# Gated linear attention: keys and queries of a tile in one strip, and score products on 64 rows

## The chip, the cores and the metric

The kernel runs on one core of a Trainium2 chip. The metric is device time in microseconds (us): the time of one launch on that core, as a median over runs. The core's engines are named as the profile names them: PE (TensorE; PEld is its weight load), DVE (VectorE), ACT (ScalarE), POOL (GpSimd) and SP (SyncE, which here only issues transfers).

## What is computed

One layer of a streaming encoder over 1024 prompt frames and 64 frames of a running stream: a normalisation with conditioning, one input projection, two groups of heads side by side (latent attention and gated linear attention), an output projection and a feed-forward block. The change lies in the gated linear attention, of 4 heads with 64 key columns each. Its reference, for a chunk of tokens (`b` is the running sum of the logarithms of the forget gates):

```
    def step(state, xs):
        qc, kc, vc, ac = xs
        b = jnp.cumsum(ac, axis=1)
        decay = jnp.exp(jnp.where(causal, b[:, :, None] - b[:, None, :], -jnp.inf))
        scores = jnp.einsum('bthk,bshk,btshk->bths', qc, kc, decay)
        o = (jnp.einsum('bths,bshv->bthv', scores, vc)
             + jnp.einsum('bthk,bhkv->bthv', qc * jnp.exp(b), state))
```

The decay depends on the query t, the key s and the column k at once, so that the scores are no plain matrix product. Between a key s and a later query t with any reference token m between them, the decay is exp(b[t] - b[m]) times exp(b[m] - b[s]), and each factor can be put on one operand.

## The kernel before, in words

**Tiles and levels.** `gla()` works through nine tiles: eight of 128 prompt tokens and one of the 64 sample frames. In a tile the pairs (s, t) with s < t are covered by levels with half-widths hf = 64, 32, 16, 8, 4, 2, 1 (seven levels, six in the sample tile). In a level the tile is cut into blocks of 2*hf tokens; the keys are the first half of each block, the queries the second half, and the reference token is the last of the first half. A level's matmuls multiply all keys of the tile with all queries of the level, and a predicated copy with a mask of the level takes the valid pairs out of the bank into the score tile `ST`. The diagonal is put in by L698 to L703.

**One level before.** `prep(hf)` makes the operands: the difference for keys on DVE (L659) and that for queries on POOL (L660), one exponential over both on ACT (L661), then the keys' product on DVE into `KL` (L664) and the queries' product into `QL` (L668), for the 64 rows of even heads on DVE and for the 64 rows of odd heads on POOL. Two heads lie on the 128 rows of an operand (the index c tells which two). `QL` is block-structured: its free half j holds the queries of head j on that head's 64 rows and zeros on the others. So one matmul over all 128 rows (L722) gives both heads' scores side by side: 128 columns of weights (the keys), 128 moving columns (2 heads by 64 queries), two such matmuls a level, into one bank `g`. One predicated copy of 128x256 (L725) takes them out. An fp32 matmul stands in the trace as two records of PE and two of PEld.

**Order.** The code is written as generators (`gla`, `main`, `latents`, `gates`, the weight loader) that `interleave` steps in turn by rough costs given in the yields; the framework then schedules each engine's program, so that the order on an engine follows from neither alone. An engine works strictly in its order. Operands are prepared two levels ahead (`ready`), a tile's first two levels during the tile before (`begin`). `KL`, `QL` and `dd` have three buffers, the PSUM pools `g` (`psG`) and `tp` (`psT`) two banks each. `tp` serves transposes: of the gate inputs (L573), of the decayed keys (L733), of the outputs (L780).

**Beside it.** While `gla()` runs, `main()` gives PE the big projections: mm3 (L93 to L95) is a product of split fp32 operands in three matmuls, with 264 to 384 moving columns. The gates' logits come from a small matmul over 33 rows (L578). The running state is updated in L739 to L750, the output made in L762 and L766. The elementwise product `qe` (L706) is on POOL.

**Where q and k come from.** `qk()` computes the projections A0 (queries) and A1 (keys) and ACT writes them to `gqk` (L498 to L514), laid out as four strips of all tokens: two of queries, two of keys.

Of the kernel before, what the change touches and what calls it, by code (L numbers as in the profile page):

```python
# [19 lines left out]
P = 128  # L20
# [51 lines left out]
def layer(ctx: ExitStack, tc: tile.TileContext, I, O):  # L72
# [202 lines left out]
    with ExitStack() as sctx:  # L275
# [208 lines left out]

        def qk():
            c0, cn = CHUNKS[0]
            banks = [(2 * g + m, g, m, mm_bank()[:, :cn]) for g in range(2) for m in range(2)]
            for hf in range(2):
                for i, g, m, ps in banks:
                    yield 0, 0, has(f"half {hf} {g}", f"h 0 {hf}")  # L490
                    wh, wl = groups[f"A{g}"]
                    ms = slice(P * m, P * m + P)
                    for kt in range(4 * hf, 4 * hf + 4):
                        mm3(ps, wh[:, kt, ms], wl[:, kt, ms], h["h"][:, kt, c0:c0 + cn], h["l"][:, kt, c0:c0 + cn],
                            kt == 0, kt == KT - 1)
                        yield 480, 0, None
                    if hf:
                        ACT.activation(gqk[0][:, i, c0:c0 + cn], ps, AF.Copy, scale=0.125 if g == 0 else 1.0)  # L498
            done.add("qk 0")
            for c, (c0, cn) in list(enumerate(CHUNKS))[1:]:  # L500
                for g in range(2):
                    yield 600, 1000, has(f"A{g}", f"h {c}", *(["shift"] if c == 2 else []))
                    scale = 0.125 if g == 0 else 1.0
                    for m in range(2):
                        ps = yield from columns(f"A{g}", m, c0, cn + (2 if c == 2 else 0))
                        qk = gqk[0][:, 2 * g + m]
                        if c < 2:
                            ACT.activation(qk[:, c0:c0 + cn], ps, AF.Copy, scale=scale)
                            continue
                        add = xp.tile([P, 2], F32, name="add", bufs=2)  # L510
                        DVE.tensor_scalar(out=add, in0=ps[:, cn:], scalar1=scale, scalar2=None, op0=ALU.mult)
                        for s, a, b in spans(c):
                            ACT.activation(qk[:, a:b], ps[:, a - c0:b - c0], AF.Identity, bias=add[:, s:s + 1], scale=scale)
                        DVE.tensor_scalar(out=qk[:, 0:c0], in0=qk[:, 0:c0], scalar1=add[:, 0:1], scalar2=None, op0=ALU.add)  # L514
# [8 lines left out]
    with gctx:  # L523
# [19 lines left out]
        KL = [big.tile([P, 2, P], F32, name=f"KL{j}") for j in range(3)]  # L543
        QL = [big.tile([P, 2, 2, 64], F32, name=f"QL{j}") for j in range(3)]
        SBk = [big.tile([P, 2, 256], F32, name=f"SB{i}") for i in range(3)]
        for t in KL + QL + SBk:
            POOL.memset(t, 0.0)
# [87 lines left out]
        def gla():  # L635
# [3 lines left out]
            def begin(i):  # L639

                off, n = TILES[i]
                q = gqk[:, 0:2, off:off + n]
                k = gqk[:, 2:4, off:off + n]
                b = bcum[:, :, off:off + n]

                def role(ap, r, hf):
                    return ap.rearrange("p c (b r h) -> p c b r h", r=2, h=hf)[:, :, :, r]

                def flat(ap, hf):
                    return ap.rearrange("p c (b h) -> p c b h", h=hf)  # L650

                def prep(hf):
                    nonlocal rot
                    nb = n // (2 * hf)
# [3 lines left out]
                    h2 = n // 2  # L658
                    DVE.tensor_tensor(out=flat(ee[:, 0, :, :h2], hf), in0=ref, in1=bs, op=ALU.subtract)  # L659
                    POOL.tensor_tensor(out=flat(ee[:, 1, :, :h2], hf), in0=bt, in1=ref, op=ALU.subtract)  # L660
                    ACT.activation(ee[:, :, :, :h2], ee[:, :, :, :h2], AF.Exp, scale=1.0 / 16)  # L661
                    kl, ql = KL[rot % 3], QL[rot % 3]
                    rot += 1
                    DVE.tensor_tensor(out=role(kl[:, :, :n], 0, hf), in0=role(k, 0, hf), in1=flat(ee[:, 0, :, :h2], hf),  # L664
                                      op=ALU.mult)
                    for j in range(2):
                        ps = slice(64 * j, 64 * j + 64)
                        (POOL if j else DVE).tensor_tensor(out=flat(ql[ps, :, j, :h2], hf), in0=role(q[ps], 1, hf),  # L668
                                           in1=flat(ee[ps, 1, :, :h2], hf), op=ALU.mult)
                    return kl, ql, nb  # L670
# [15 lines left out]
            for i, (off, n) in enumerate(TILES):  # L686
# [19 lines left out]
                POOL.tensor_tensor(out=qe[:, :, :n], in0=q, in1=E1[:, :, :n], op=ALU.mult)  # L706
# [3 lines left out]
                for lv, hf in enumerate(halves):  # L710
                    kl, ql, nb = ready.pop(0)
# [7 lines left out]
                    sc = g_bank()  # L719
                    scv = sc.rearrange("p (c j t) -> p c j t", c=4, j=2)[:, 0:2]  # L720
                    for p in range(2):
                        PE.matmul(scv[:n, p, :, :n // 2], lhsT=kl[:, p, :n], rhs=ql[:, p, :, :n // 2],  # L722
                                  start=True, stop=True)
                    mlv = 6 - (hf.bit_length() - 1)
                    DVE.copy_predicated(  # L725
                        ST[:n, :, :n].rearrange("p c (b r h) -> p c b r h", r=2, h=hf)[:, :, :, 1],
                        masks[:n, mlv, :n // 2].rearrange("p (o b h) -> p o b h", o=1, h=hf).broadcast_to([n, H, nb, hf]),
                        scv[:n].rearrange("p c j (b h) -> p (c j) b h", h=hf)[:, :, :nb])
# [1114 lines left out]
```

## Time and profile before

| | |
|---|---|
| median of 3 runs | 1420.18 us (1418.73 to 1422.01) |
| the profiled execution | 1419.29 us, of which the span of its instructions is 1417.5 us |
| PE busy | 1349.8 us (95%) |
| DVE busy | 873.6 us (62%) |
| ACT busy | 655.6 us (46%) |
| POOL busy | 273.1 us (19%) |
| levels of the linear attention on PE (L722) | first at 106.0 us, last at 269.1 us of the span |

The shares of the whole span say little on this change: the linear attention lies between about 100 and 280 us of 1417.5, and the rest of the kernel is projections, the latent attention and a long feed-forward part. The views to read are therefore those cut to that stretch. A PE record runs from its start to the end of its results, and records overlap, so that the distance between two starts, not a record's duration, is what a matmul costs in a dense row. PE counts as busy in the tail of a lone record too.

### The profile page before, as it was taken

To read this page: it belongs to the slowest core of one execution; us is meant where nothing else is said; L and a number is where in the kernel's file an instruction comes from. 1 tells how busy PE (TensorE), PEld (TensorE's weight loads), DVE (VectorE), ACT (ScalarE), POOL (GpSimd) and SP (SyncE) were. 2 spreads that over 40 slices of the span, in tenths; PEclk is the share of its full clock that TensorE was granted. 3 is DMA by queue.
4 is the path that set the end of the run, shared out by engine and by line. 5 is a ranking of instruction groups with operands and counts; after the bars stand their busy time and mean duration, and the time that the engine had idled before them with its cause. 6 is when DMAs were issued, how large, how long until landed. Compare 5 with 4: busy or idle time off the path is not lost.

```text
span 1417.5 us, 26453 instructions
## 1 busy us (share of the span) xinstructions
PE 1349.8 (95%) x10014; PEld 1263.6 (89%) x10014; DVE 873.6 (62%) x1894; ACT 655.6 (46%) x1623; POOL 273.1 (19%) x388
## 2 busy tenths in 40 slices
PE   6988899988999999999987999999999999999998
PEld 5888788886866778899986999999999999999998
DVE  5678777336455665654489665665544776774554
ACT  5455454335335566653455544444444333333332
POOL 3155445213121211013564000000000000000000
PEclk9999999999999999999998999999999999999999
DMA  9320021384243442164224534444437864533440
GB/s 347 109 72 9 16 72 55 107 235 129 84 142 123 157 120 71 44 204 135 80 76 125 182 132 140 156 140 131 141 113 271 324 221 152 185 114 108 127 126 33
DMA packets 165594, 188.17 MB, mean 133 GB/s; under 512 B 16814, under 2 KB 116442, under 8 KB 165466
## 3 DMA queue, kind: packets, MB, share of 16 engines
q1 hardware_dynamic: 158010, 180.90, 40.0%
q10 hardware_dynamic: 7456, 5.57, 1.2%
q8 instruction: 79, 1.29, 0.4%
q14 instruction: 49, 0.40, 0.1%
HBM read 132.97 MB, written 53.46 MB: 132 GB/s over the span
## 4 chain that ended last, share of the span: by engine, by line
PE 77%; DVE 10%; DMA 4%; POOL 3%; ACT 3%; issue 2%; SPq 0%; DVEq 0%; POOLq 0%; ACTq 0%
PE mm L93 13%; PE mm L94 13%; PE mm L95 13%; PE g L93 6%; PE g L95 6%; PE g L94 5%; PE mm L964 3%; PE tp L93 3%; PE tp L95 3%; PE tp L94 3%; PE g L991 2%; PE mm L166 2%; DMA raw<-in_w_in 1%; PE tp L1001 1%; DMA gv<-mix_d 1%
## 5 line engine op out<-in xcount | busy, mean ns | idle before, releaser
L101 ACT CAST opers<-quad 128x512 fp32r<-128x512 f32 x112 | 69.4, 620 | 184.6 <-PE mm L95 145.3
L102 DVE TENSOR_TENSOR opers<-quad,opers 128x512 fp32r<-128x512 f32 x112 | 77.1, 689 | 112.6 <-ACT opers L101 112.6
L93 PE MATMUL mm<-ah,wh 128*128 128x272 f32 x424 | 123.0, 291 | 6.2 <-ACT st L1565 6.2
L93 PE MATMUL mm<-opers 128*128 128x272 f32 x448 | 128.6, 287 | 0.3 <-DVE e L1775 0.3
L95 PE MATMUL mm<-opers 128*128 128x272 f32 x448 | 128.9, 288 | 0.0
L94 PE MATMUL mm<-opers 128*128 128x272 f32 x448 | 128.3, 286 | 0.0
L95 PE MATMUL mm<-ah,wl 128*128 128x272 f32 x424 | 122.7, 290 | 1.0 <-POOL wl L102 1.0
L94 PE MATMUL mm<-al,wh 128*128 128x272 f32 x424 | 122.8, 290 | 0.0
L93 PE MATMUL mm<-hh,wh 128*128 128x384 f32 (+2 forms) x264 | 90.6, 346 | 0.6 <-ACT hh L101 0.5
L94 PE MATMUL mm<-hl,wh 128*128 128x384 f32 (+2 forms) x264 | 87.6, 333 | 0.0
L95 PE MATMUL mm<-hh,wl 128*128 128x384 f32 (+2 forms) x264 | 87.2, 331 | 0.0
L93 PEld LDWEIGHTS mm<-ah,wh 128*128 128x128 f32 x424 | 81.2, 192 | 6.5 <-ACT st L1565 6.4
L93 PEld LDWEIGHTS mm<-opers 128*128 128x128 f32 x448 | 84.6, 189 | 0.5 <-issue 0.5
L95 PEld LDWEIGHTS mm<-opers 128*128 128x128 f32 x448 | 84.3, 188 | 0.0
L94 PEld LDWEIGHTS mm<-opers 128*128 128x128 f32 x448 | 84.1, 188 | 0.0
L95 PEld LDWEIGHTS mm<-ah,wl 128*128 128x128 f32 x424 | 80.7, 191 | 1.2 <-POOL wl L102 1.2
L94 PEld LDWEIGHTS mm<-al,wh 128*128 128x128 f32 x424 | 80.9, 191 | 0.0
L102 DVE TENSOR_TENSOR opers<-ru,opers 128x544 fp32r<-128x544 f32 x108 | 77.5, 719 | 2.2 <-ACT opers L101 2.0
L101 ACT CAST opers<-ru 128x544 fp32r<-128x544 f32 x108 | 69.3, 643 | 13.1 <-PE mm L95 11.7
L101 ACT CAST wh<-ru 128x512 fp32r<-128x512 f32 x67 | 41.1, 618 | 70.9 <-PE g L94 26.0
L93 PE MATMUL mm<-wh,hh 128*128 128x264 f32 (+3 forms) x216 | 66.4, 307 | 1.6 <-ACT wh L213 1.6
L94 PE MATMUL mm<-wl,hh 128*128 128x264 f32 (+3 forms) x216 | 65.6, 304 | 0.9 <-DVE wl L105 0.9
(415 smaller groups left out, 4434.6 us busy)
## 6 DMA issues: line engine op xcount, KB each, us to landing
ru<-u_d SPq DMA_DIRECT2D x108, 272.0 KB, 2.8
raw<-in_w_ada SPq DMA_DIRECT2D x40, 512.0 KB, 3.9
ru<-in_w_up SPq DMA_DIRECT2D x32, 512.0 KB, 4.1
quad<-in_w_down SPq DMA_DIRECT2D x16, 1024.0 KB, 7.6
u_d<-st SPq DMA_DIRECT2D x60, 272.0 KB, 2.1
u_d<-sc SPq DMA_DIRECT2D x45, 272.0 KB, 2.2
raw<-in_w_in SPq DMA_DIRECT2D x22, 256.0 KB, 3.0
x<-in_xo_T SPq DMA_DIRECT2D x8, 544.0 KB, 5.1
```

The lines of the kernel that those rows point to most:

```text
L93: PE.matmul(out, lhsT=ah, rhs=bh, start=first, stop=False, skip_group_check=more)
L94: PE.matmul(out, lhsT=ah, rhs=bl, start=False, stop=False, skip_group_check=more)
L95: PE.matmul(out, lhsT=al, rhs=bh, start=False, stop=last, skip_group_check=more)
L101: ACT.copy(hi, src)
L102: eng.tensor_tensor(out=lo, in0=src, in1=f32(hi), op=ALU.subtract)
L166: mm = PE.matmul(acc[32 * j:32 * j + 32, 0:256], lhsT=scT[:, k, :], rhs=was[k][:, 256 * j:256 * (j + 1)], start=(k == 0), stop=(k == KT - ...
L964: PE.matmul(sp[:n, :w], lhsT=x[:, hd, :n], rhs=y[:, hd, :w], start=(j == 0), stop=(j == 4))
L991: PE.matmul(op[:n, 0:P], lhsT=pt[:kw, k, :n], rhs=kvs[kt // 4].v[:kw, kt % 4, hd], start=(kt == 0), stop=(kt == nkt - 1))
L1001: PE.transpose(tp[:kw, k, :n], pr[k0 // 4][:n, P * k:P * k + kw], ident[:n, :n])
```

## The change

Four things are changed, all in the linear attention and in the place of its operands:

1. `gqk` is laid out by tiles: for a tile of n tokens a strip of 4n elements, with the keys of two heads, the keys of the other two, and then the queries likewise. `qk()` writes through views by tiles (`qk_place`, `by_tile`), with the same instructions.
2. In `prep`, one difference over the whole tile (DVE, 128x256) takes the place of two of 128x128. The exponential becomes two instructions on ACT, one with a scale of -1/16 for the keys' halves and one with 1/16 for the queries' halves, each of 128x128. One product on DVE makes keys and queries of all heads into `KQ`, by a view (`roles`) that walks the keys' first halves and the queries' second halves: 128x256 of the 128x512 elements of a tile. `KL` and `QL`, with its zeros, are gone, and so is POOL's part. In L710 `qe` goes from POOL to DVE.
3. A level's scores are multiplied for each head by itself: for j = 0 on rows 0 to 63 into a `g` bank, for j = 1 on rows 64 to 127 into a `tp` bank, two matmuls each (128 columns of weights, 64 moving columns). Four matmuls of 64 rows take the place of two of 128 rows.
4. Each bank is taken out by a predicated copy of its own (128x128), two in place of one. In the first level (one block) ACT copies the valid 64 rows of each bank without a mask.

In the sample tile all token counts are halved.

The diff, cut to its core:

```
-            gqk.append(gqkp.tile([P, 4, TOK], F32, name="gqk"))
+            gqk.append(gqkp.tile([P, 4 * TOK], F32, name="gqk"))
...
+        def qk_place(r, a, b):
+            if a == SEQ:
+                return gqk[0][:, 4 * SEQ + DEC * r:4 * SEQ + DEC * r + DEC]
+            return gqk[0][:, 4 * a:4 * b].rearrange("p (i r t) -> p r i t", r=4, t=P)[:, r]
...
-                    bs, bt = role(b, 0, hf), role(b, 1, hf)
-                    ref = bs[:, :, :, hf - 1:hf].broadcast_to([P, 2, nb, hf])
-                    ee = gw.tile([P, 2, 2, 64], F32, name="dd", bufs=3)
-                    DVE.tensor_tensor(out=flat(ee[:, 0, :, :h2], hf), in0=ref, in1=bs, op=ALU.subtract)
-                    POOL.tensor_tensor(out=flat(ee[:, 1, :, :h2], hf), in0=bt, in1=ref, op=ALU.subtract)
-                    ACT.activation(ee[:, :, :, :h2], ee[:, :, :, :h2], AF.Exp, scale=1.0 / 16)
-                    kl, ql = KL[rot % 3], QL[rot % 3]
+                    bv = b.rearrange("p c (x y) -> p c x y", y=2 * hf)
+                    ref = bv[:, :, :, hf - 1:hf].broadcast_to([P, 2, n // (2 * hf), 2 * hf])
+                    ee = gw.tile([P, 2 * P], F32, name="dd", bufs=3)[:, 0:2 * n]
+                    DVE.tensor_tensor(out=ee.rearrange("p (c x y) -> p c x y", c=2, y=2 * hf), in0=bv, in1=ref, op=ALU.subtract)
+                    ev = ee.rearrange("p (x r h) -> p r x h", r=2, h=hf)
+                    for r in range(2):
+                        ACT.activation(ev[:, r], ev[:, r], AF.Exp, scale=(-1.0 / 16, 1.0 / 16)[r])
+                    out = KQ[rot % 3][:, 0:4 * n]
...
-                    DVE.tensor_tensor(out=role(kl[:, :, :n], 0, hf), in0=role(k, 0, hf), in1=flat(ee[:, 0, :, :h2], hf),
-                                      op=ALU.mult)
-                    for j in range(2):
-                        ps = slice(64 * j, 64 * j + 64)
-                        (POOL if j else DVE).tensor_tensor(out=flat(ql[ps, :, j, :h2], hf), in0=role(q[ps], 1, hf),
-                                           in1=flat(ee[ps, 1, :, :h2], hf), op=ALU.mult)
+                    DVE.tensor_tensor(out=roles(out, hf), in0=roles(kq, hf), in1=ev, op=ALU.mult)
...
-                POOL.tensor_tensor(out=qe[:, :, :n], in0=q, in1=E1[:, :, :n], op=ALU.mult)
+                DVE.tensor_tensor(out=qe[:, :, :n], in0=q, in1=E1[:, :, :n], op=ALU.mult)
...
-                    sc = g_bank()
-                    for p in range(2):
-                        PE.matmul(scv[:n, p, :, :n // 2], lhsT=kl[:, p, :n], rhs=ql[:, p, :, :n // 2],
-                                  start=True, stop=True)
-                    DVE.copy_predicated(
...
+                    for j, bank in enumerate((g_bank(), tp_bank())):
+                        ks = kq[64 * j:64 * j + 64]
+                        sc = bank[:, 0:P].rearrange("p (c t) -> p c t", c=2)
+                        for p in range(2):
+                            PE.matmul(sc[:n, p, :n // 2].rearrange("p (b h) -> p b h", h=hf), lhsT=ks[:, n * p:n * p + n],
+                                      rhs=ks[:, 2 * n + n * p:3 * n + n * p].rearrange("p (b r h) -> p r b h", r=2, h=hf)[:, 1],
+                                      start=True, stop=True)
...
+                        if nb == 1:
+                            ACT.copy(to[:hf], sc[:hf])
+                            continue
+                        DVE.copy_predicated(to, masks[:n, mlv, :n // 2].rearrange("p (o b h) -> p o b h", o=1, h=hf)
+                                            .broadcast_to([n, 2, nb, hf]), sc)
```

How the built programs differ is shown at two places. The rows are in an engine's order, a line and an operation each, with what is written and read, and "x2" where two such stand together. First PE in the first tile, at its first two levels. Before: `g` is the bank of a level, `QL` and `KL` are its operands, `mm` a projection.

```order
L95 MATMUL mm<-wh,hl 128x264
L722 MATMUL g<-QL_906,KL_903 128x128 x2
L93 MATMUL mm<-wh,hh 128x264
L94 MATMUL mm<-wl,hh 128x264
L95 MATMUL mm<-wh,hl 128x264
...
L733 MATMUL tp<-ident,kk 128x128 x2
L93 MATMUL mm<-wh,hh 128x264
L722 MATMUL g<-QL_907,KL_904 128x128 x2
L94 MATMUL mm<-wl,hh 128x264
```

At the same place after the change (L728 is the new line of the scores, L585 that of the gate input's transpose, L743 that of the decayed keys):

```order
L728 MATMUL g<-KQ_903 128x64 x2
L93 MATMUL mm<-wh,hh 128x264
L94 MATMUL mm<-wl,hh 128x264
L585 MATMUL tp<-ident,gl 16x128
L728 MATMUL tp<-KQ_903 128x64 x2
L95 MATMUL mm<-wh,hl 128x264
...
L743 MATMUL tp<-ident,kk 128x128 x2
L93 MATMUL mm<-wh,hh 128x264
L728 MATMUL g<-KQ_904 128x64 x2
L728 MATMUL tp<-KQ_904 128x64 x2
L94 MATMUL mm<-wl,hh 128x264
```

The first level's two halves stand apart, with projection matmuls between them, the second level's stand together. In all, the 112 matmuls of the eight prompt tiles stood in 48 runs between other matmuls, and the 224 that take their place stand in 66.

Then DVE, in the second tile, around its first levels. Before (`dd` are the differences, `ST` the score tile):

```order
L725 COPY_PREDICATED ST<-masks,g 128x4x64
L664 TENSOR_TENSOR KL_904<-gqk,dd 128x16x8
L668 TENSOR_TENSOR QL_907<-gqk,dd 64x2x64
L659 TENSOR_TENSOR dd<-bcum 128x128
L725 COPY_PREDICATED ST<-masks,g 128x8x32
L664 TENSOR_TENSOR KL_905<-gqk,dd 128x32x4
L668 TENSOR_TENSOR QL_908<-gqk,dd 64x2x64
L725 COPY_PREDICATED ST<-masks,g 128x16x16
```

After (L667 is the difference, L673 the product, L737 the predicated copy):

```order
L673 TENSOR_TENSOR KQ_904<-gqk,dd 128x2x16x8
L667 TENSOR_TENSOR dd<-bcum 128x256
L737 COPY_PREDICATED ST<-masks,g 128x2x2x32
L737 COPY_PREDICATED ST<-masks,tp 128x2x2x32
L673 TENSOR_TENSOR KQ_905<-gqk,dd 128x2x32x4
L737 COPY_PREDICATED ST<-masks,g 128x2x4x16
L737 COPY_PREDICATED ST<-masks,tp 128x2x4x16
```

A level had four instructions on DVE and two on POOL; it has four on DVE (two in the first level) and none on POOL.

More of the change, by code (lines that the diff above doesn't have):

```diff
@@ L497, in qk @@
                     if hf:
-                        ACT.activation(gqk[0][:, i, c0:c0 + cn], ps, AF.Copy, scale=0.125 if g == 0 else 1.0)
+                        ACT.activation(qk_place((i + 2) % 4, c0, c0 + cn), by_tile(ps, c0), AF.Copy,
+                                       scale=0.125 if g == 0 else 1.0)
             done.add("qk 0")
@@ L641, in begin, with roles @@
                 off, n = TILES[i]
-                q = gqk[:, 0:2, off:off + n]
-                k = gqk[:, 2:4, off:off + n]
+                kq = gqk[:, 4 * off:4 * off + 4 * n]
+                k, q = (kq[:, 2 * n * r:2 * n * r + 2 * n].rearrange("p (c t) -> p c t", c=2) for r in range(2))
                 b = bcum[:, :, off:off + n]
[L646 to L650, printed above, removed]
+                def roles(t, hf):
+                    return bass.AP(t.tensor, t.offset, [list(t.ap[0]), [2 * n + hf, 2], [2 * hf, n // hf], [1, hf]])
```

31 lines of the change are left out of this document (15 added, 16 removed).

## The prediction

> **What bounds the kernel now.** I read first the busy time of the engines in stretches of 20 us over the linear attention, because the shares of the whole span mix it with projections and the feed-forward part. Columns: PE, PEld, DVE, ACT and POOL busy, with instructions in brackets, then PE's granted clock and the DMA share.
>
> ```profile
> 100.00:120.00 20.00, 16.19 (x110) 13.77 (x109) 16.69 (x54) 12.48 (x41) 11.02 (x21) 1.00 0.05 18
> 120.00:140.00 20.00, 18.94 (x132) 17.67 (x133) 16.13 (x49) 10.52 (x42) 12.36 (x23) 0.91 0.05 15
> 140.00:160.00 20.00, 18.64 (x137) 16.78 (x136) 12.28 (x37) 4.95 (x13) 3.44 (x8) 1.00 0.05 14
> 160.00:180.00 20.00, 15.62 (x97) 13.48 (x96) 17.77 (x55) 13.09 (x52) 14.59 (x26) 0.91 0.05 14
> 180.00:200.00 20.00, 17.27 (x129) 15.41 (x128) 17.73 (x56) 9.87 (x33) 13.29 (x25) 1.00 0.12 32
> 200.00:220.00 20.00, 17.90 (x118) 15.59 (x117) 14.74 (x43) 10.75 (x35) 6.06 (x11) 1.00 0.40 121
> 220.00:240.00 20.00, 19.23 (x128) 17.95 (x127) 17.45 (x56) 10.25 (x36) 13.25 (x25) 1.00 0.10 33
> 240.00:260.00 20.00, 20.00 (x130) 18.63 (x128) 11.13 (x33) 8.08 (x27) 5.18 (x13) 1.00 0.45 141
> ```
>
> PE is the busiest engine in most stretches; DVE is close to it, and ahead of it in 100 to 120 and in 160 to 200. PE's idle time in the eight is 16.2 us (20 less busy, added up). That is the most that shorter waits can give back by themselves. The same view, for the score matmuls L722 alone (PE, PEld):
>
> ```profile
> 100.00:120.00 20.00, 4.73 (x28) 3.73 (x28) 1.00 0.05 18
> 120.00:140.00 20.00, 5.39 (x36) 4.59 (x36) 0.91 0.05 15
> 140.00:160.00 20.00, 3.27 (x20) 2.82 (x20) 1.00 0.05 14
> 160.00:180.00 20.00, 6.20 (x36) 5.41 (x36) 0.91 0.05 14
> 180.00:200.00 20.00, 5.66 (x36) 4.72 (x36) 1.00 0.12 32
> 200.00:220.00 20.00, 2.74 (x16) 2.20 (x16) 1.00 0.40 121
> 220.00:240.00 20.00, 5.56 (x36) 4.80 (x36) 1.00 0.10 33
> 240.00:260.00 20.00, 3.33 (x24) 2.87 (x24) 1.00 0.45 141
> ```
>
> A level has four records, so these are 7, 9, 5, 9, 9, 4, 9 and 6 levels, the last two of the six being of the sample tile. What a level costs PE where nothing is waited for stands in the timeline of PE:
>
> ```profile
> 246.09 0.31 PE L94 MATMUL mm<-hl,wh 128*128 128x320 f32 x1
> 246.24 0.32 PE L95 MATMUL mm<-hh,wl 128*128 128x320 f32 x1
> 246.40 0.61 PE L722 MATMUL g<-QL,KL 128*128 128x128 f32 x4
> 246.76 0.39 PE L93 MATMUL mm<-hh,wh 128*128 128x320 f32 x1
> 246.99 0.31 PE L94 MATMUL mm<-hl,wh 128*128 128x320 f32 x1
> ```
>
> From L95 to the second L94 it is 0.75 us, of which the two projection matmuls take 0.15 each (246.09 to 246.24 is one such step): 0.45 us a level. In the table a level is busy for longer than that; the excess is the tail of a level after which PE waits, so time that is free too. Free time per stretch, idle plus (L722 busy less 0.45 a level): 5.4, 2.4, 2.4, 6.5, 4.3, 3.0, 2.3 and, with the two sample levels at a little more, 0.4 us: 26.7 us.
>
> **The change on PE.** Each half of a level has two matmuls, so four records, as a whole level had before. They have 64 moving columns in place of 128. What fewer moving columns give is shown by L698, also four records with 128 columns of weights:
>
> ```profile
> 101.79 0.53 PE L698 MATMUL g<-indi,pr 128*128 128x2 f32 x4
> 102.18 0.36 PE L93 MATMUL mm<-wh,hh 128*128 128x264 f32 x1
> ```
>
> With 2 moving columns it holds PE from 101.79 to 102.18, 0.39 us; L722 above, with 128, from 246.40 to 246.76, 0.36. The weights' 128 columns set the pace, and half the moving columns save nothing: a half level by itself costs 0.45 us. The Trainium skill (TensorEngine Tiling (Array Packing), Instruction Overhead) puts a matmul's floor at about 60 cycles of moving columns and so would let the halves come at about half price; the row does not bear that out, and by the rule the later sum of 50 us would be about 25.
>
> Next, the switch of PE to 64 rows and back. L578, on 33 rows, is such a visit, with four records of 128 weight columns and 256 moving ones; L739 is the same on all 128 rows:
>
> ```profile
> 110.69 0.28 PE L95 MATMUL mm<-wh,hl 128*128 128x264 f32 x1
> 110.81 0.28 PE L93 MATMUL mm<-wh,hh 128*128 128x264 f32 x1
> 111.02 1.13 PE L578 MATMUL g<-glrT,wg 33*128 33x256 f32 x4
> 112.08 0.39 PE L94 MATMUL mm<-wl,hh 128*128 128x264 f32 x1
> 112.30 0.28 PE L95 MATMUL mm<-wh,hl 128*128 128x264 f32 x1
> ...
> 198.35 1.03 PE L739 MATMUL g<-gv,kt__2153 128*128 128x256 f32 x4
> 199.22 0.61 PE L722 MATMUL g<-QL,KL 128*128 128x128 f32 x4
> ```
>
> From L93 to the second L95 it is 1.49 us; less two projection matmuls at 0.12 (110.69 to 110.81) it is 1.25. On all rows the same records take 199.22 - 198.35 = 0.87. A visit costs 0.38 us beside its work. The order has 66 runs of the new score matmuls among the eight prompt tiles: 66 x 0.38 = 25.1 us. The Trainium skill (TensorEngine Tiling (Array Packing), Key Properties) says that changing the tiling mode drains PE while changing the tile does not; the 0.38 us agrees with the first half. Were each of the 112 halves a switch of its own, the sum would be 46 x 0.38 = 17.5 us higher.
>
> Do two halves that stand together run at once, being on different rows and banks? No row here shows it for rows. The nearest is for columns: L166 has four matmuls on four groups of 32 columns, eight records with 256 moving columns.
>
> ```profile
> 57.29 0.64 PE L166 MATMUL mm<-raw,scT 128*32 128x256 f32 x8
> 57.86 0.44 PE L93 MATMUL mm<-hh,wh 128*128 128x384 f32 x1
> ```
>
> They are done in 0.57 us, where L739's pace (0.87 / 4) would take 1.74. So groups run side by side, and that is the nearer end. Then 54 runs of two or four matmuls cost 0.45 each, and the other 70 matmuls, in 12 longer or odd runs, 0.45 for each four: 24.3 + 7.9 = 32.2 us, against 56 x 0.45 = 25.2 before: 7 us more. One after the other it is 112 x 0.45 = 50.4, so 25 us more. I take side by side: PE gets 25.1 + 7 = 32 us more, 0.57 a level (0.90 if in turn, 50 us in all).
>
> **DVE, POOL, ACT.** DVE's four instructions a level in the prompt tiles (busy us, mean ns), and then shortest, median and longest of some lines:
>
> ```profile
> L725 DVE COPY_PREDICATED ST<-masks,g 128x256 f32<-128x256 int32 x56 | 28.9, 516 | 6.2 <-PE g L722 5.3 <-ACT og L771 0.4
> L664 DVE TENSOR_TENSOR KL<-gqk,dd 128x128 f32<-128x128 f32 x56 | 20.5, 365 | 0.1
> L668 DVE TENSOR_TENSOR QL<-gqk,dd 64x128 f32<-64x128 f32 x56 | 19.6, 351 | 0.0
> L659 DVE TENSOR_TENSOR dd<-bcum 128x128 f32<-128x128 f32 x56 | 19.5, 370 | 1.3 <-POOL QL L668 1.2
> ...
> L659 DVE TENSOR_TENSOR dd<-bcum x62: 224/278/826, 102.5 to 250.2; 128x128 f32<-128x128 f32 x56, 128x64 f32<-128x64 f32 x6
> ...
> L673 DVE TENSOR_TENSOR pr<-gqk x9: 273/408/668, 89.8 to 232.6; 128x256 f32<-128x256 f32 x8, 128x128 f32<-128x128 f32 x1
> L725 DVE COPY_PREDICATED ST<-masks,g x62: 284/438/742, 106.8 to 269.4; 128x256 f32<-128x256 int32 x56, 64x128 f32<-64x128 int32 x6
> ...
> L661 ACT ACTIVATE dd<-dd x62: 309/417/462, 103.2 to 253.2; 128x256 f32<-128x256 f32 x56, 128x128 f32<-128x128 f32 x6
> ```
>
> Before: 88.5 us. After: a difference and a product of 128x256 at 0.41 each (L673's median), two copies of 128x128 in 48 levels, between 0.22 (half of 0.438) and 0.44, taken at 0.30, the sample tile's shortest being 0.284; and eight `qe` at 0.41 from POOL. 56 x 0.82 + 48 x 0.60 + 3.3 = 78 us: 10 us less (18 less to 3 more by the ends). Nothing of this is booked as a gain, since PE has the more to do; it is why I let PE use all of its free time. POOL's two operations a level go, and with them what was waited for there; late next is DVE's product behind ACT. ACT gets two exponentials of half the size for one, about 0.31 each (the shortest of L661, of that size) for 0.42, and two copies a tile. It is busy for 5 to 13 of 20 us, and operands are prepared two levels ahead, so I book nothing; were that cover gone, 62 x 0.2 = 12 us. `qk()` issues the same instructions through other views: nothing. No transfer is moved.
>
> **The sum.** In each stretch PE's extra work (0.57 a level) less its free time, where positive: 0, 2.7, 0.5, 0, 0.8, 0, 2.9 and 1.9 us: 8.8 us (in the last, four prompt levels). The sample tile's six levels had 64 columns of weights and get eight records for four: up to half a level's 0.45 each, about 1 us in all. Together +10 us: 1419.3 (the profiled execution, with a span of 1417.5) becomes 1429. That execution lies 0.9 us under the median of the runs; so 1430 on that scale.
>
> **The rivals.** *In turn.* PE's order puts all of one half ahead of the other, and 128 columns of weights may not load on two row groups at once. Extra 0.90 a level; by the same stretches 0.9, 5.7, 2.1, 1.6, 3.8, 0.6, 5.8, 3.2 and 1.5 for the sample tile: +25 us, 1445. With none of the free time used it is 1419 + 52 = 1471. Against it is L166's row.
>
> *Faster: the vector side sets the pace, and PE's additions fall into waits.* In 160 to 200 DVE is busy for 35.5 of 40 us and POOL for 27.9. If the level's chain through both is what PE waits for, DVE's 10 us and POOL's part come off it, and a switch costs nothing where PE stands still anyway. It decides if PE's extra is under the free time of 26.7 us, 0.48 a level, where I have 0.57. All idle time gone would be -16.2, so 1403; half of it, 1411. For it: much of the free time lies where the levels are densest. Against it: 120 to 140 and 220 to 260 have next to none. The Trainium skill (SBUF — State Buffer, Who interferes with whom) says that a DVE instruction with two inputs in SBUF contends with a GpSimd instruction that reads SBUF; the trace agrees (L659: 370 ns in the mean, 278 in the median). By that rule DVE's excess over the medians, some 0.09 x 4 x 56 = 20 us, would go with POOL's work.
>
> *No change.* Extra work and free time balance if half of the switches fall into waits (33 x 0.38 = 12.5 less): -2, so about 1417 to 1422.
>
> *Banks.* Levels now share the two `tp` banks with the transposes L573, L733 and L780, three groups in each of nine tiles. If each of the 27 waits about 1 us for copies queued on DVE (two of them and a product), it is +27 on top, 1457. Against it: `g` was shared in the same way.
>
> That the change doesn't do what it says is no case: the orders show POOL's operations gone and the halves in two banks.
>
> **How the numbers follow.** Forecast (side by side; +6 if all free time is used anywhere, +20 if half of it is): 0.44. In turn: 0.32. Faster: 0.13. No change: 0.06. Banks: 0.05. The predicted time is the forecast's, 1430 us. The range, 1411 to 1455, runs from the faster rival's middle to well over the second case, and leaves out the ends beyond. A measurement can tell about 0.2%, 2.8 us, from no change: faster 0.13, same 0.07, slower 0.80, one part in a hundred of "same" being the forecast's low edge.
>
> **What would show it.** Right: the stretch of the levels ends at about 280 to 290 us in place of 269; L728 groups with about 0.38 us around them; PE at 20 of 20 in most stretches; DVE about 10 us less busy; POOL nearly empty. Side by side shows as eight records in about 0.45 us, in turn as eight in 0.9. Wrong: a span under 1414, the levels ending before 265 us, or PE idle for longer than before.

## The result, and the profile after

| | before | after |
|---|---|---|
| median of the runs, us (lowest to highest, runs) | 1419.45 (1417.42 to 1422.01, 4) | 1431.97 (1429.12 to 1434.12, 4) |
| ratio, 95% interval | | 1.0086 (1.006 to 1.0112) |
| profiled execution, us (span) | 1419.29 (1417.5) | 1429.12 (1427.2) |
| PE busy over the span, us (idle) | 1349.8 (67.7) | 1374.7 (52.5) |
| PE records | 10014 | 10262 |
| DVE, ACT, POOL busy over the span, us | 873.6, 655.6, 273.1 | 864.9, 664.1, 203.3 |
| last score matmul, us from the span's start | 269.1 | 280.6 |

The change makes the kernel 12.5 us slower, where 10 to 11 had been forecast. First, as for before, the busy time of the engines in stretches of 20 us, in the kernel after (columns as in the prediction):

```profile
100.00:120.00 20.00, 19.53 (x147) 17.01 (x146) 14.58 (x52) 12.90 (x49) 0.00 (x0) 1.00 0.05 15
120.00:140.00 20.00, 19.84 (x156) 17.24 (x156) 14.42 (x47) 12.77 (x58) 2.41 (x4) 1.00 0.05 14
140.00:160.00 20.00, 20.00 (x146) 17.02 (x146) 9.76 (x33) 4.92 (x15) 0.00 (x0) 1.00 0.05 14
160.00:180.00 20.00, 18.76 (x130) 15.86 (x130) 15.79 (x53) 12.15 (x51) 1.25 (x2) 0.91 0.05 14
180.00:200.00 20.00, 20.00 (x126) 16.56 (x126) 12.56 (x39) 9.68 (x42) 1.20 (x2) 0.84 0.05 15
200.00:220.00 20.00, 20.00 (x138) 16.65 (x138) 13.84 (x41) 8.83 (x33) 1.62 (x2) 1.00 0.35 95
220.00:240.00 20.00, 19.60 (x143) 16.70 (x142) 17.17 (x55) 12.11 (x50) 1.34 (x2) 1.00 0.23 69
240.00:260.00 20.00, 20.00 (x145) 17.93 (x143) 11.08 (x37) 9.10 (x42) 1.20 (x2) 1.00 0.15 48
```

PE's idle time in the eight stretches was 16.2 us and is 2.3. DVE is ahead of PE nowhere any more. POOL, which had up to 14.59 us of work in such a stretch, has at most 2.41. PE has used up nearly all of its free time and still needs 11.5 us longer to the last score matmul.

What PE does in a level, in the timeline of PE of the same kernel (start, duration, engine, line). The first piece is a half that stands alone, the second a level whose two halves stand together:

```profile
209.81 0.28 PE L95 MATMUL mm<-wh,hl 128*64 128x264 f32 x1
210.02 0.66 PE L728 MATMUL g<-KQ 64*128 64x64 f32 x4
210.60 0.33 PE L93 MATMUL mm<-wh,hh 128*64 128x264 f32 x1
210.77 0.28 PE L94 MATMUL mm<-wl,hh 128*64 128x264 f32 x1
...
257.10 0.31 PE L95 MATMUL mm<-hh,wl 128*128 128x320 f32 x1
257.34 0.32 PE L728 MATMUL g<-KQ 64*128 64x64 f32 x1
257.35 0.32 PE L728 MATMUL tp<-KQ 64*128 64x64 f32 x1
257.50 0.27 PE L728 MATMUL g<-KQ 64*128 64x64 f32 x1
257.52 0.27 PE L728 MATMUL tp<-KQ 64*128 64x64 f32 x1
257.62 0.27 PE L728 MATMUL g<-KQ 64*128 64x64 f32 x1
257.63 0.27 PE L728 MATMUL tp<-KQ 64*128 64x64 f32 x1
257.73 0.27 PE L728 MATMUL g<-KQ 64*128 64x64 f32 x1
257.74 0.27 PE L728 MATMUL tp<-KQ 64*128 64x64 f32 x1
257.94 0.41 PE L93 MATMUL mm<-hh,wh 128*128 128x320 f32 x1
258.19 0.31 PE L94 MATMUL mm<-hl,wh 128*128 128x320 f32 x1
```

In the second piece the records of `g` (upper rows) and `tp` (lower rows) start 10 to 20 ns apart, though the program has both matmuls of one half ahead of both of the other: they run side by side. From L95 to the L94 behind it is 1.09 us, less two projection steps of 0.145 it is 0.80 us; a level before took 0.45. The lone half takes 210.77 - 209.81 = 0.96, less two steps of 0.12 (210.77 is followed by 210.89), so 0.72; the median of 17 such is 0.79. A half alone costs PE nearly as much as both together, and either costs 0.3 to 0.35 us more than the 0.45 of a level on 128 rows.

DVE's instructions between 98 and 295 us of the kernel after (busy us, mean ns, idle time ahead and its releaser):

```profile
L667 DVE TENSOR_TENSOR dd<-bcum 128x256 f32<-128x256 f32 x56 | 23.1, 422 | 0.2
L673 DVE TENSOR_TENSOR KQ<-gqk,dd 128x256 f32<-128x256 f32 x56 | 23.0, 421 | 0.8 <-ACT dd L670 0.5
L737 DVE COPY_PREDICATED ST<-masks,tp 128x128 f32<-128x128 int32 x48 | 17.2, 358 | 7.3 <-PE tp L728 5.9 <-PE g L728 1.2
L737 DVE COPY_PREDICATED ST<-masks,g 128x128 f32<-128x128 int32 x48 | 16.4, 342 | 11.2 <-PE tp L728 7.9 <-PE g L728 2.9
...
L710 DVE TENSOR_TENSOR qe<-gqk,E 128x256 f32<-128x256 f32 x8 | 3.4, 424 | 6.2 <-PE mm L772 6.1
```

They come to 83.1 us, where before had 88.5. DVE now waits for PE's scores (the copies' idle time), while the score matmuls wait for DVE's products for only 1.3 us between 100 and 300 us.

### The profile page after: what moved, and what is told of

Its sections match the earlier page's. It is cut to its first block, busy times and chain, and to the rows that moved or that the text cites. A ratio compares the mean times of both kernels' runs of the same rounds, so it can differ in the third digit from the quotient of the medians.

```text
span 1427.2 us, 26776 instructions
## 1 busy us (share of the span) xinstructions
PE 1374.7 (96%) x10262; PEld 1279.3 (90%) x10262; DVE 864.9 (61%) x1885; ACT 664.1 (47%) x1703; POOL 203.3 (14%) x252
## 4 chain that ended last, share of the span: by engine, by line
PE 82%; DVE 7%; DMA 4%; ACT 2%; POOL 2%; issue 2%; SPq 1%; DVEq 0%; POOLq 0%; ACTq 0%
PE mm L93 14%; PE mm L95 13%; PE mm L94 13%; PE g L95 5%; PE g L93 5%; PE g L94 5%; PE mm L974 3%; PE tp L93 3%; PE tp L95 3%; PE tp L94 3%; PE g L1001 2%; PE g L728 2%; PE mm L166 2%; DMA raw<-in_w_in 1%; DMA gv<-mix_d 1%
## 5 line engine op out<-in xcount | busy, mean ns | idle before, releaser
L95 PE MATMUL mm<-opers 128*128 128x272 f32 x448 | 128.9, 288 | 0.0
L94 PE MATMUL mm<-opers 128*128 128x272 f32 x448 | 128.3, 286 | 0.0
L95 PE MATMUL mm<-ah,wl 128*128 128x272 f32 x424 | 123.1, 291 | 0.9 <-POOL wl L102 0.9
L94 PE MATMUL mm<-al,wh 128*128 128x272 f32 x424 | 123.1, 291 | 0.0
L94 PE MATMUL mm<-hl,wh 128*128 128x384 f32 (+2 forms) x264 | 87.8, 333 | 0.0
L95 PE MATMUL mm<-hh,wl 128*128 128x384 f32 (+2 forms) x264 | 87.5, 332 | 0.0
L95 PEld LDWEIGHTS mm<-opers 128*128 128x128 f32 x448 | 84.3, 188 | 0.0
L94 PEld LDWEIGHTS mm<-opers 128*128 128x128 f32 x448 | 84.1, 188 | 0.0
L95 PEld LDWEIGHTS mm<-ah,wl 128*128 128x128 f32 x424 | 81.0, 191 | 1.2 <-POOL wl L102 1.2
L94 PEld LDWEIGHTS mm<-al,wh 128*128 128x128 f32 x424 | 81.3, 192 | 0.0
L93 PE MATMUL mm<-wh,hh 128*128 128x264 f32 (+3 forms) x216 | 67.7, 314 | 1.6 <-ACT wh L213 1.6
L94 PE MATMUL mm<-wl,hh 128*128 128x264 f32 (+3 forms) x216 | 65.6, 304 | 0.9 <-DVE wl L105 0.9
```

The costliest lines, as they stand in the source:

```text
L93: PE.matmul(out, lhsT=ah, rhs=bh, start=first, stop=False, skip_group_check=more)
L94: PE.matmul(out, lhsT=ah, rhs=bl, start=False, stop=False, skip_group_check=more)
L95: PE.matmul(out, lhsT=al, rhs=bh, start=False, stop=last, skip_group_check=more)
```

## The experiments

The theory: the 64-row scores cost PE about 0.35 us for each visit to 64 rows, the halves run side by side, and what the vector side gives back is mostly hidden behind PE. The rivals: 64 rows are not the cost but the vector side or the shared banks are; or the halves pay in turn. Ten variants were run beside before, in three groups: rows_alone, visit64, visit128 and wide_dve with before at 1420.07 us; wide_pool, together, pair and quad at 1421.05; rows_together and pinned, made for what the first eight left open, at 1419.74.

One column has to be explained ahead. Each run lists the mean clock that PE was granted over the span, and the variants differ in it, as the section on rows_alone shows. "Time by clock" is the mean over a variant's runs of time times that clock: roughly what the run would have taken had the clock been full throughout. It is not exact, since PE time at half clock in which PE would have waited anyway is no loss, and a clock is listed to three digits, which is 0.7 us either way for a single run. Before has 1400.6, 1400.4 and 1401.7 in the three groups. "Idle" is PE's idle time from 100 to 340 us of the profiled execution, "runs" how often the order goes from other matmuls to score matmuls, the sample tile included. The last score matmul, in us from the span's start, shows where the levels end, but it is no measure of the time: quad has the earliest and is still slower than before.

| | runs | median, us | ratio (95%) | clock | time by clock | idle, us | last score matmul |
|---|---|---|---|---|---|---|---|
| before | 54 | 1420.07 | | 0.986 | 1400.6 | 25.1 | 269.1 |
| after | 72 | 1431.97 | 1.0086 (1.006 to 1.0112) | 0.985 | 1410.3 | 8.1 | 280.6 |
| visit64 | 53 | 1432.77 | 1.0088 (1.0071 to 1.0105) | 0.987 | 1414.3 | 14.2 | 284.9 |
| visit128 | 53 | 1425.94 | 1.0037 (1.0025 to 1.005) | 0.986 | 1406.2 | 20.7 | 274.5 |
| rows_alone | 69 | 1448.32 | 1.0197 (1.0178 to 1.0216) | 0.974 | 1411.1 | 5.9 | 297.3 |
| rows_together | 66 | 1434.28 | 1.0108 (1.0089 to 1.0128) | 0.980 | 1406.6 | 18.7 | 282.4 |
| wide_dve | 56 | 1422.54 | 1.002 (1.0008 to 1.0032) | 0.983 | 1399.2 | 24.4 | 271.4 |
| wide_pool | 53 | 1415.12 | 0.9955 (0.994 to 0.997) | 0.986 | 1394.9 | 20.4 | 265.5 |
| together | 63 | 1423.77 | 1.002 (1.0005 to 1.0034) | 0.984 | 1400.6 | 13.2 | 271.2 |
| pinned | 66 | 1431.7 | 1.0076 (1.0057 to 1.0094) | 0.980 | 1403.2 | 9.8 | 280.4 |
| pair | 38 | 1429.91 | 1.0061 (1.0042 to 1.008) | 0.979 | 1400.5 | 20.4 | 260.5 |
| quad | 21 | 1428.23 | 1.0057 (1.0038 to 1.0076) | 0.979 | 1399.4 | 27.2 | 255.5 |

### visit64 and visit128: the visit by itself

Before, with one idle matmul of two moving columns added to each level, on 64 rows (visit64) or on all 128 (visit128):

```
+ PE.matmul(sc[:n, 256:258], lhsT=kl[0:64, 1, :n], rhs=ql[0:64, 1, 0, 0:2], start=True, stop=True)   # visit64
+ PE.matmul(sc[:n, 256:258], lhsT=kl[:, 1, :n], rhs=ql[:, 1, 0, 0:2], start=True, stop=True)   # visit128
```

> The kernel before with one idle matmul a level added behind the scores: 64 rows, 128 weight columns, 2 moving columns, into unused columns of the bank; nobody reads it. Theory: 0.22 us of work and 0.35 us for a visit, in each of 53 runs, so about 32 us more PE work, and no relief elsewhere: 1429 to 1438 us. Rival (visits fall into waits): within 3 us of before.

> The same idle matmul as in the run with 64 rows, but on 128 rows: the work of 0.22 us a level without the visit. Theory: 14 us more PE work, of which the free time takes most: 1419 to 1425 us, and at least 8 us under the run on 64 rows. Rival: the same as the run on 64 rows.

A level in the timeline of PE, in visit64:

```profile
243.20 0.31 PE L95 MATMUL mm<-hh,wl 128*128 128x320 f32 x1
243.35 0.61 PE L722 MATMUL g<-QL,KL 128*128 128x128 f32 x4
243.89 0.38 PE L724 MATMUL g<-QL,KL 64*128 64x2 f32 x2
244.20 0.42 PE L93 MATMUL mm<-hh,wh 128*128 128x320 f32 x1
244.46 0.32 PE L94 MATMUL mm<-hl,wh 128*128 128x320 f32 x1
```

And in visit128:

```profile
250.72 0.32 PE L95 MATMUL mm<-hh,wl 128*128 128x320 f32 x1
250.87 0.61 PE L722 MATMUL g<-QL,KL 128*128 128x128 f32 x4
251.32 0.28 PE L724 MATMUL g<-QL,KL 128*128 128x2 f32 x2
251.46 0.39 PE L93 MATMUL mm<-hh,wh 128*128 128x320 f32 x1
251.69 0.31 PE L94 MATMUL mm<-hl,wh 128*128 128x320 f32 x1
```

From L95 to the L94 behind it is 1.26 us with 64 rows and 0.97 with 128: the same two records cost 0.29 us more as a visit. With 53 runs that is 15 us of PE; the medians differ by 6.8 us (8.1 by clock), and PE's idle time is 6.5 us less. So a visit is paid where PE is busy and vanishes where PE would wait. visit64 lies in its range; the 6.8 is under the 8 that was expected, and visit128 is just above its range: two more records a level (0.97 less 0.30 is 0.67, against 0.45) are not free either.

### rows_alone: scores on 64 rows, operands as before

Before with the change's 64-row scores, two banks and two copies, and its own differences, products and POOL work:

```
-                        PE.matmul(scv[:n, p, :, :n // 2], lhsT=kl[:, p, :n], rhs=ql[:, p, :, :n // 2],
-                                  start=True, stop=True)
+                    for j, bank in enumerate((g_bank(), tp_bank())):
+                        ps = slice(64 * j, 64 * j + 64)
+                        sc = bank[:, 0:P].rearrange("p (c t) -> p c t", c=2)
+                        for p in range(2):
+                            PE.matmul(sc[:n, p, :n // 2], lhsT=kl[ps, p, :n], rhs=ql[ps, p, j, :n // 2], start=True, stop=True)
...
```

> The kernel before with one part of the change: the scores on 64 rows into two banks with two copies a level; operands as before (DVE and POOL). Theory (PE pays for its visits to 64 rows, 0.35 us each, and both halves run side by side): 69 runs of score matmuls, 31 us more PE work as in the changed kernel, and no relief for DVE, so 1430 to 1440 us. Rival (the new vector work and its longer chain cost the time, the visits fall into waits): at most 5 us over before, 1419 to 1424.

Slower than every expectation: 1448.32. The busy time of the engines in stretches of 4 us shows why (the column behind POOL is PE's granted clock):

```profile
178.00:182.00 4.00, 3.51 (x28) 3.05 (x28) 3.36 (x12) 2.06 (x7) 1.15 (x3) 1.00 0.16 46
182.00:186.00 4.00, 3.82 (x22) 3.43 (x20) 4.00 (x16) 1.16 (x4) 2.59 (x5) 0.61 0.08 22
186.00:190.00 4.00, 4.00 (x15) 3.16 (x14) 1.25 (x5) 1.31 (x8) 2.68 (x3) 0.50 0.00 0
...
206.00:210.00 4.00, 4.00 (x23) 3.30 (x23) 1.43 (x7) 2.39 (x5) 0.76 (x2) 0.50 0.00 0
210.00:214.00 4.00, 4.00 (x19) 3.92 (x19) 3.57 (x13) 0.69 (x2) 0.70 (x2) 0.55 0.00 0
214.00:218.00 4.00, 4.00 (x34) 3.43 (x33) 0.92 (x3) 3.46 (x18) 2.81 (x5) 1.00 0.46 135
```

From about 183 to 214 us PE is busy all the time and runs at half its clock: 15 to 23 records in 4 us in place of 34. That one stretch loses 15.4 us (the sum of 1 less clock over its microseconds). The trace is of one run, but all four have the low mean clock, 0.972 to 0.975, so that it seems to belong to this order of work and not to one execution. By clock rows_alone is at 1411.1, which at before's clock of 0.986 would be 1431 us, inside the 1430 to 1440 expected; the other 17 of its 28 us are put down to the clock. The Trainium skill (TensorE: Matmul & The Clock Gate, What's actually happening) says that PE's clock is gated to half after an idle window of about 3.4 us and full again after a busy one. The trace agrees with the half (0.50) and with the size of the window: short dips lose 1.7 us each, half of 3.4, in before as in the variants. It doesn't agree that busy PE lifts the gate within a window: here it stayed shut for 31 us at a busy share of 4.00 in 4. Nor does an idle window stand ahead of each dip: in the 3.4 us ahead of this stretch PE was busy for 80% by the profile, and ahead of a short dip of the same trace, at 138.5 us, for all of them. Which activity counts is not settled here; what ran in the stretch were mainly scores on 64 rows, the output's small matmuls and projections with 64 weight columns in place of 128.

### rows_together: is it the stretch at half clock?

rows_alone, with the four matmuls of a level held together in the order and alternating between the halves:

```
+ for j, p in ((1, 0), (0, 0), (1, 1), (0, 1)):
+     ps = slice(64 * j, 64 * j + 64)
+     sc = banks[j][:, 0:P].rearrange("p (c t) -> p c t", c=2)
+     mm = PE.matmul(sc[:n, p, :n // 2], lhsT=kl[ps, p, :n], rhs=ql[ps, p, j, :n // 2], start=True, stop=True)
+     if p or not j:
+         tc.keep_in_program_order(mm)
```

> The operands, differences and POOL's work of before; scores on 64 rows as in rows_alone, but the four matmuls of a level alternate between the halves and are held together in the order (66 runs in place of 69, and fewer levels split in two). In rows_alone the trace shows PE at half its clock from 182 to 214 us, and its runs' mean clock is 0.974 where before has 0.986; its time by its clock is 1411, after's 1410, before's 1400. Theory (64 rows cost the same with the old operands as with the new ones, the rest of rows_alone's excess is that stretch at half clock): time by clock 1402 to 1410, the clock back at 0.982 to 0.987 where the long stretch is gone, so 1420 to 1434. Rival (64 rows on the old operands are dearer by themselves, whatever the clock): 1438 or more, or time by clock over 1413. Undecided on the clock: if the long stretch stays, 1436 to 1446 with time by clock still under 1410.

1434.28, at the upper end of the theory's range (0.3 us over it); by clock 1406.6, inside it. In the profiled run, with a clock of 0.982, the long stretch is gone: there are only dips that lose 1.7 to 5.1 us each. It can't be said of all runs: two of the six, at 1439 us, have a clock of 0.975 and 0.976, and no trace of them was kept. The mean clock is 0.980, a little under what was expected. Of the 14 us that it is under rows_alone, 4.5 are work and about 9 the clock. By clock, 64 rows with the old operands cost 5 us here (1406.6 less the group's 1401.7): the rival, that old operands make them dearer, needed over 1413 by clock and falls by that measure.

### wide_dve and wide_pool: the vector part alone

After, with the scores on 128 rows as before. One difference a level, two exponentials of half the size, `qe` on DVE as in after; the products are apart again, since `QL` needs its zeros, the queries' product for odd heads is on POOL in wide_pool (shown) and on DVE in wide_dve, and a level has one bank and one copy again:

```
-                    DVE.tensor_tensor(out=roles(out, hf), in0=roles(kq, hf), in1=ev, op=ALU.mult)
+                    DVE.tensor_tensor(out=kl.rearrange("p (x r h) -> p r x h", r=2, h=hf)[:, 0],
+                                      in0=kq[:, 0:2 * n].rearrange("p (x r h) -> p r x h", r=2, h=hf)[:, 0], in1=ev[:, 0], op=ALU.mult)
+                    for j in range(2):
+                        ps = slice(64 * j, 64 * j + 64)
+                        (POOL if j else DVE).tensor_tensor(
+                            out=ql[ps, :, j, :n // 2].rearrange("p c (b h) -> p c b h", h=hf),
+                            in0=q[ps].rearrange("p c (b r h) -> p r c b h", r=2, h=hf)[:, 1],
+                            in1=ee[ps].rearrange("p (c b r h) -> p r c b h", c=2, r=2, h=hf)[:, 1], op=ALU.mult)
```

> The changed kernel with the scores on 128 rows as before: one difference on DVE, two exponentials, nothing on POOL, but the products made apart (keys, queries of even heads, queries of odd heads, all on DVE) for the block-structured operand; one bank, one copy. DVE gets about 0.13 us a level more than in the changed kernel, PE no visits. Theory: PE's 31 us go and POOL's waits stay away: 1404 to 1417 us, under before. Rival: DVE has more to do than in the changed kernel, so not under it: 1432 or more.

> The run on 128 rows with the products made apart, but with the queries of odd heads on POOL as before: DVE 0.28 us a level less, POOL 0.46 us a level back. Theory: PE as before, DVE lightest of all: 1404 to 1415 us, within 4 us of the run with all on DVE. Rival: not under the changed kernel.

wide_pool is faster than both kernels, 1415.12, at the upper end of its range (0.1 us over it). wide_dve, at 1422.54, is not even under before, against the expectation. The stretch from 160 to 180 us, where DVE is densest, in wide_dve:

```profile
160.00:180.00 20.00, 14.98 (x87) 12.94 (x86) 17.68 (x60) 11.94 (x50) 1.30 (x2) 0.87 0.05 14
```

And in wide_pool:

```profile
160.00:180.00 20.00, 16.76 (x96) 14.81 (x95) 16.32 (x51) 13.49 (x60) 7.31 (x14) 0.83 0.05 14
```

With the third product on DVE, PE does 87 records there, with POOL's help 96. In the waits of PE between 100 and 260 us, the scores' wait for a product is 4.4 us in wide_dve and 1.0 in wide_pool:

```profile
PE g L731 <- DVE QL L674: 4.4, 4, 1.3
```

```profile
PE g L731 <- DVE QL L674: 1.0, 1, 1.0
```

So with 128-row scores the vector side does set PE's pace in places, and the change's vector part is worth 5.5 us by clock (1400.4 less 1394.9; 5.9 in the medians), if POOL keeps a share of the products. The two differ by 7.4 us where up to 4 was expected; by clock it is 4.3.

### together and pinned: the order inside a level

After, with a level's four matmuls held behind one another: in together they alternate between the halves, in pinned they stand in after's sequence. Other matmuls can still come between them.

```
+ for j, p in ((1, 0), (0, 0), (1, 1), (0, 1)):      # pinned: ((0, 0), (0, 1), (1, 0), (1, 1))
+     ks = kq[64 * j:64 * j + 64]
+     sc = banks[j][:, 0:P].rearrange("p (c t) -> p c t", c=2)
+     mm = PE.matmul(sc[:n, p, :n // 2].rearrange("p (b h) -> p b h", h=hf), lhsT=ks[:, n * p:n * p + n],
+                    rhs=ks[:, 2 * n + n * p:3 * n + n * p].rearrange("p (b r h) -> p r b h", r=2, h=hf)[:, 1], start=True, stop=True)
+     if p or not j:      # pinned: if j or p
+         tc.keep_in_program_order(mm)
```

> The changed kernel with a level's four score matmuls written alternately (odd heads, even heads, odd, even) and each kept behind the one ahead of it in PE's order: 63 runs in place of 72. Theory: 9 visits fewer, 3 us: 1427 to 1431 us. Rival: no difference from the changed kernel, 1430 to 1434.

> After with one edit: a level's four matmuls are held together in the order, in after's own sequence (both of one half, then both of the other); together has the same with the halves alternating. It has 66 runs where after has 72 and together 63, the sample tile's among them. Theory (what together gained is that fewer levels are split, since a half alone costs a visit of its own and as long as both; the sequence inside a level does not matter because the halves run side by side in either): like together, time by clock 1400 to 1405, so 1422 to 1430 at clocks of 0.982 to 0.986. Rival (alternating is what pays): like after, time by clock 1409 or more, 1430 to 1436.

together is 8 us faster than after, more than was expected; by clock it is level with before. The order of after has 31 runs of two matmuls, each a half alone in the trace, and a level that is split costs PE a second 0.79 us; together has 9 runs fewer, 7 us. It has no half alone any more, though nine single matmuls still stand apart. In pinned 17 halves alone are left of the 31. It has 6 runs fewer than after and is 7 us under it by clock (1403.2, inside the theory's range), but loses that again to the clock: its runs have 0.979 to 0.982, at or below the low end of what was expected, and its time, 1431.7, is after's and lies in the rival's range. The rival, that alternating is what pays, has the time for it and the time by clock against it; that the sequence matters little is shown by that measure alone, and why pinned gets the lower clock stays open. The 12 runs of together show what the clock is worth within one program: from 1418.34 us at a clock of 0.988 to 1428.57 at 0.980.

### pair and quad: fewer visits

After, with two (pair) or four (quad) levels in one pair of banks, so that their matmuls follow one another; four or five `KQ` buffers. Some small tiles share buffers, to make room.

```
+ groups = [halves[a:a + 2] for a in range(0, len(halves), 2)]        # quad: 4
+ banks = [bank.rearrange("p (l c t) -> p l c t", l=4, c=2) for bank in (g_bank(), tp_bank())]
```

> The changed kernel with two levels sharing a pair of banks and their eight score matmuls kept in one run, four KQ buffers for three (the space comes from sharing a buffer between og and mog, and between pr and kt): 38 runs in place of 72. Theory: 34 visits fewer, 12 us of PE work: 1419 to 1425 us. Rival: two levels have to be ready before PE may begin, the chain is longer: 1432 or more.

> The same with four levels to a pair of banks and their sixteen matmuls in one run; five KQ buffers, two dd buffers; the next group's operands are made after the matmuls of this one: 21 runs. Theory: 51 visits fewer, 18 us of PE work, the rest as in the changed kernel: 1412 to 1420 us, at or under before. Rival: PE waits for four levels' operands at a time: 1435 or more.

Both miss their ranges, and their rivals' too: 25 and 42 visits fewer than together, at 0.35 us 9 and 15 us, and nothing of it in the time. PE's sums over 100 to 340 us (the first figure, of 240.00, is PE's busy time), in together:

```profile
sum 240.00, PE 226.80 PEld 198.31 DVE 141.92 ACT 114.53 POOL 24.42; mean PE 18.90 PEld 16.53 DVE 11.83 ACT 9.54 POOL 2.03
```

In pair:

```profile
sum 240.00, PE 219.56 PEld 197.43 DVE 137.76 ACT 110.49 POOL 22.45; mean PE 18.30 PEld 16.45 DVE 11.48 ACT 9.21 POOL 1.87
```

In quad, with two of its stretches of 4 us:

```profile
172.00:176.00 4.00, 0.58 (x4) 0.49 (x5) 3.97 (x15) 1.81 (x8) 0.00 (x0) 0.78 0.25 70
...
216.00:220.00 4.00, 0.97 (x5) 0.82 (x4) 3.82 (x14) 3.26 (x12) 0.00 (x0) 0.50 0.36 104
...
sum 240.00, PE 212.77 PEld 194.64 DVE 137.07 ACT 110.54 POOL 22.17; mean PE 17.73 PEld 16.22 DVE 11.42 ACT 9.21 POOL 1.85
```

PE's idle time rises by 7 and 14 us against together: what the visits no longer take, PE waits. In quad 12.5 us of its waits between 100 and 260 us are for DVE's `qe` and for `ST`. Whether the groups or the shared buffers make it wait was not separated. In quad's two stretches DVE is busy for nearly all of 4 us, with the operands and copies of a whole group, and PE for less than one. In and behind each of the two gaps the clock falls to 0.50. The mean clock of 0.979 against together's 0.984 is another 7 us.

## Why the prediction was right, point by point

**The free time.** It was the ground of the sum that PE would use all of its free time and pay only the rest. PE idles 2.3 us in place of 16.2 in the eight stretches, and the levels end at 280.6 us, at the lower end of the 280 to 290 named.

**The visit.** Taken at 0.38 us from one gate matmul on 33 rows, it measured 0.3 to 0.35 in after and 0.29 in visit64 against visit128. 66 visits are 19 to 23 us in place of 25.1.

**Side by side.** Taken from a row on column groups, it holds for row groups: eight records in 0.80 us with the visit in it, about 0.45 without. In turn, which had 0.32 of the chance, is excluded: it needed 0.90 without the visit.

**Moving columns.** Half as many saved nothing: a half alone costs 0.72 to 0.79 us, the 0.45 of four records on 128 rows and the visit.

**The sum.** PE's extra work, estimated by the order's runs at 0.79 for a half, 0.80 for a level and more for the longer ones, is about 33 us where 32 were booked. The profiled execution came to 1429.12 where 1429 was forecast; the runs' median is 1.97 us over the 1430. That it fits to a microsecond owes something to luck, as the next points show: a gain from the vector side and a loss to the clock were both left out, and 1 us was booked for the sample tile that was not there.

**The vector side.** "Nothing of this is booked as a gain" is the step that was wrong, though it did little harm. DVE got 83.1 us of such work, not 78, since the copies took 0.35 us in place of 0.30. But wide_pool shows that a vector part of this kind is worth 5.5 us by clock as long as the scores stay on 128 rows. On 64 rows it depends on the order: with a level's matmuls held together it is 4.7 us (rows_together is 4.9 over its before, together 0.2), in the scheduler's order under 1 (rows_alone is 10.5 over its before, after about 9.7). So 64 rows cost more than the forecast's 10 where the new vector part is in place: from wide_pool to after it is 15.4 us by clock, from wide_dve to after 11. With the old operands it is 10.5 (rows_alone) or 5 (rows_together). The rival in which the vector side sets the pace had its mechanism right in part; it did not decide because its condition was not met: PE's extra work, about 33 us, was over the free time of 26.7.

**The order.** The forecast took its runs from the built order and booked 0.45 us and a visit for each, for a half alone as for a whole level, so the price of a split level was in its sum and holds. What it did not ask is how much of the sum is the scheduler's doing. together, which changes the order alone, is 8.2 us under after in the medians and 9.7 by clock; pinned is level with after in the medians and 7.1 under it by clock. So most of the loss lies in how the scheduler placed the halves, and not in 64 rows as such. together shows it in the time, pinned only by clock.

**Small terms.** The sample tile's 1 us was not there: eight records take 0.553 us where four took 0.567. The banks rival is excluded: PE's idle time between 100 and 300 us comes to 2.3 us in all.

**The clock.** The forecast had no term for it. In after it is a small one: 0.985 against 0.986, about 1.5 of the 12.5 us. In rows_alone, rows_together, pinned, pair and quad it is 9 to 17 us, and without it they could not have been read.

## What to carry to other kernels

Price a change to PE's row groups as visits: count in the built order how often PE goes from full rows to fewer and back, take the price of one from a row that already does it, and subtract the time in which PE stands idle in that stretch alone. Halves of a level are worth having only if they stand together, since a half alone costs as much as both. When a variant's time makes no sense, read PE's granted clock ahead of anything else: pinned lost at half clock what it saved in work. What in an edit brings that on is not shown here.

## What was not expected of the hardware

- PE's granted clock fell to 0.50 and stayed there for 31 us, with PE busy throughout (rows_alone, 183 to 214 us); a projection step takes 0.22 us there in place of 0.12. Other dips of these traces last 3.4 to 13.7 us and lose 1.7 us or a multiple. What opens the gate again stays open.
- Matmuls on the two row halves start 10 to 20 ns apart even when the program has both of one half ahead of both of the other (after, 257.34 to 257.94 us; pinned, where that sequence is held, 257.19 to 257.59 us). So PE does not start matmuls on different rows strictly in the program's order.
- Four fp32 records with 128 columns of weights take 0.45 us with 128 moving columns on 128 rows, and two with 2 moving columns add 0.22 (visit128): up to 128 moving columns it is the records that cost, not the columns. With 256 moving columns four take 0.87 (L739).
